# Softmax normalisation moved from the probabilities to a head pair's result, through DRAM; second query copies on GpSimd; squares of projections from SBUF

## The chip, the core and the metric

The kernel runs on one core of a Trainium2 chip. The metric is the device time of one execution in microseconds (us). A core has five engines with queues of their own that run in order: TensorE (PE in the profile, its weight loads PEld), VectorE (DVE), ScalarE (ACT), GpSimd (POOL) and SyncE (SP, which here only issues DMAs). They meet through semaphores. SBUF and PSUM are the on-chip memories; DRAM is reached by DMA alone.

## What is computed

Two layers of a streaming encoder over 512 tokens of width 1024. Each layer is a feed-forward block, a mixer and another feed-forward block. The mixer projects its input, runs two attention branches of 8 heads (A with a position bias, C with a forget bias) and a pooling branch, gates them and projects back. What matters here is one head of an attention branch:

```
logits = jnp.einsum('bqhd,bkhd->bhqk', qb, kf) + (cq[..., None] - cum_k[:, :, None, :])
logits = jnp.where(mask[None, None], logits, NEG_INF)
p = jax.nn.softmax(logits, axis=-1).astype(v.dtype)
return jnp.einsum('bhqk,bkhd->bqhd', p, v)
```

`qb` and `kf` are projections divided by their root mean square over the 64 elements of a head, so the squares of the projections are summed too.

## The kernel before, in words

All matrix products are made three times from values split into a high and a low part (`triple`, L117 to L122): a raw block comes in by DMA (`raw`), ACT writes the high part `whi` (L271), DVE the low part `wlo` (L273). Two raw buffers and three of `whi` and of `wlo` rotate. Tiles are taken from rings of a few buffers by tag: `t1` has 2, `t2` 3, `b` 17, PSUM has 4 banks named `mm` and 4 named `acc`. Whoever takes the next buffer of a ring waits until its last readers are done.

The program's order is made by a planner in the kernel: `later(delay, fn)` puts a task off until so many units of matmul work have been written out, and `poll` runs the tasks that are due. The order in which the instructions of each engine then stand is set when the program is built.

Attention (`attention`) goes over the heads h = 0..7, two heads to a pair p. For each head it writes four blocks of 128 queries, i = 0..3, and after each a piece of other work (`filler`): projections of branch C beside branch A, the gated merge of branch A beside branch C. One block is:

- `logits` (L945): two matmuls (L951, L952) into an `mm` bank; DVE adds bias or mask from the `strip` tile and finds the maximum (L955) into a `t1` tile; ACT takes the exponential into a `t2` tile `pr` with its row sum (L959); DVE inverts the sum (L961); `pr` is multiplied by it (L962), on POOL for i = 0..2 and on DVE for i = 3.
- `turn` (L965), 24 units later: PE transposes `pr` (L974) into an `mm` bank, ACT and DVE split it (L978, L979).
- `weigh` (L984), after each half of the queries, 14 units later: PE multiplies with the values (L996, L997); ACT copies the other half's rows into a `t1` tile (L1000), DVE adds (L1001), ACT and POOL split the sum into `y` (`split_to`, L378, L379), which a later merge multiplies.

The strips of the next head come by DMA and are finished on POOL: a memset in branch A (L926), an addition of the causal mask in branch C (L937).

Queries and keys come from `proj_qk`. As each of four PSUM banks `acc` is done, `evac` copies it (L826, ACT) and squares it (L828, ACT, from PSUM), and DVE sums the squares (L829). Later `turn` (L841) transposes one pair of heads into an `mm` bank; ACT writes the scaled rows (L853) and, for queries, writes them a second time to the other 64 partitions (L856); DVE makes the low part (L859); POOL fills the rest with zeros (L857).

Of the kernel before, what the change touches and what calls it, by code (L numbers as in the profile page):

```python
# [15 lines left out]
F32 = mybir.dt.float32  # L16
F32R = mybir.dt.float32r
I32 = mybir.dt.int32
AF = mybir.ActivationFunctionType
ALU = mybir.AluOpType  # L20
AX = mybir.AxisListType

P = 128
T = 512
# [6 lines left out]
HD = 64  # L31
NT = T // P
# [8 lines left out]
def encoder_kernel(tc, xT, c, w_ada, b_ada, gains, w_gate, w_up, w_down, w_qkv, w_f, w_ubg,  # L41
                   qk_gain, rel, fbias, w_pool, pool_scale, w_branch, w_out, inv_cnt, w_first, out):
    nc = tc.nc
# [10 lines left out]
    dr = open_pool(name="dr", bufs=1, space=bass.MemoryType.DRAM)  # L54
# [3 lines left out]
    NB, NRAW = 17, 2  # L58
# [5 lines left out]
    def st(shape, dt, tag, bufs):  # L64
        return sb.tile(shape, dt, tag=tag, bufs=bufs, name=nm(tag))
# [7 lines left out]
    def blk(tag, dt=F32R):  # L73
        bufs = {"xv": 4, "v2": 4, "b": NB}[tag]
        return st([P, 2, T], dt, tag, bufs)
# [22 lines left out]
    def later(delay, fn, group=None):  # L98
        t = Task(pe[0] + delay, fn, group)
        tasks.append(t)  # L100
        return t
# [33 lines left out]
    for b in range(4):  # L135
# [3 lines left out]
        sq = st([P, 2, T], F32, "wlo" if b else "whi", 3)  # L139
# [32 lines left out]

    x_dram = dr.tile([4, P, 2 * T], F32, name="x_dram")
    fv_dram = [dr.tile([H, FVLEN], F32, name=f"fv_dram{l}") for l in range(L)]

    last = {}

# [199 lines left out]
    def split_to(hi, lo, src, lo_eng=nc.vector):  # L377
        nc.scalar.copy(hi, src)  # L378
        lo_eng.tensor_tensor(lo, src, hi.bitcast(F32), op=ALU.subtract)  # L379
# [438 lines left out]
    def proj_qk(l, col, gcol, is_q, res, pre=None, norm=None):  # L818
        lows = []
        qs = []  # L820

        def evac(t, a):
            if t == 0:
                qs.extend((st([P, NT, T], F32, "ptb", 2), st([P, NT, H], F32, "qss", 1)))
            qn, ss = qs
            nc.scalar.copy(qn[:, t, :], a)  # L826
            sq = t2(T)
            nc.scalar.activation(sq, a, AF.Square)  # L828
            nc.vector.tensor_reduce(ss[:, t, :], sq.rearrange("p (h d) -> p h d", h=H), axis=AX.X, op=ALU.add)  # L829

        yield from proj(l, col, evac, pre, norm)
        qn, ss = qs
        v = st([P, NT * H], F32, "nt_v32", 2)
        nc.vector.tensor_scalar(v, ss.rearrange("p t h -> p (t h)"), 1.0 / HD, EPS, op0=ALU.mult, op1=ALU.add)
        r = rsqrt(v, NT * H)
        for t in range(NT):
            q3 = qn[:, t, :].rearrange("p (h d) -> p h d", h=H)
            eng = nc.vector if t % 2 else nc.gpsimd
            eng.tensor_tensor(q3, q3, r[:, t * H:(t + 1) * H].unsqueeze(2).to_broadcast([P, H, HD]), op=ALU.mult)

        def turn(p):  # L841
            pt = mmt()
            for t in range(NT):
                nc.tensor.transpose(pt[:, t * P:(t + 1) * P], qn[:, t, p * P:(p + 1) * P], ident)
            pe[0] += 2.2
            b = blk("b")
            if is_q:
                lows.append(blk("b"))
            first, second = slice(0, HD), slice(HD, P)
            for odd, (own, other) in enumerate(((first, second), (second, first))):  # L850
                dst = b[:, odd, :]
                gc = gcol[own, :]
                nc.scalar.activation(dst[own, :], pt[own, :], AF.Identity, scale=gc)  # L853
                low = dst[other, :]
                if is_q:
                    nc.scalar.activation(low, pt[own, :], AF.Identity, scale=gc)  # L856
                    nc.gpsimd.memset(lows[p][other, odd, :].bitcast(F32), 0.0)  # L857
                    low = lows[p][own, odd, :]
                nc.vector.scalar_tensor_tensor(low, pt[own, :], gc, dst[own, :].bitcast(F32),  # L859
                                               op0=ALU.mult, op1=ALU.subtract)  # L860
            res.append((b, lows[p]) if is_q else b)

        todo = [lambda p=p: turn(p) for p in range(4)]
        turns.append(todo)

        def ready(p):
            if len(todo) >= 4 - p:
                if heads[0] < (Q_GATE if is_q else K_GATE)[p]:
                    later(8, lambda: ready(p))
                else:  # L870
                    while len(todo) >= 4 - p:
                        todo.pop(0)()

        for p in range(4):
            later(TURN + 12 * p, lambda p=p: ready(p))
# [64 lines left out]
    def attention(qs, ks, vs, strip, ys, filler, budget, group):  # L940


        open_pt = {}

        def logits(h, i, strips):  # L945
            p, off = divmod(h, 2)
            (q, ql), k = qs[p], ks[p]
            odd = h % 2
            n = (i + 1) * P
            s = mmt()  # L950
            mm(s[:, :n], q[:, odd, i * P:(i + 1) * P], k[:, odd, :n], start=True, stop=False)  # L951
            mm(s[:, :n], ql[:, odd, i * P:(i + 1) * P], k[:, odd, :n], start=False, stop=True)  # L952
            lg = t1(T)[:, :n]
            mx = st([P, 1], F32, "mx", 4)
            nc.vector.tensor_tensor_reduce(out=lg, in0=s[:, :n], in1=strips[i], scale=-1.0, scalar=BIG,  # L955
                                           op0=ALU.add, op1=ALU.min, accum_out=mx)
            pr = t2(T)[:, :n]
            sm = st([P, 1], F32, "sm", 4)
            nc.scalar.activation(pr, lg, AF.Exp, bias=mx, scale=-1.0, accum_out=sm)  # L959
            rs = st([P, 1], F32, "rs", 4)  # L960
            nc.vector.reciprocal(rs, sm)  # L961
            (nc.vector if i == NT - 1 else nc.gpsimd).tensor_scalar(pr, pr, rs, None, op0=ALU.mult)  # L962
            pe[0] += 0.5 * (i + 1.5)
            later(LAG_T, lambda: turn(h, i, pr), group)

        def turn(h, i, pr):
            half, c = divmod(i, 2)
            nj = 2 * half + 2
            if c == 0:
                open_pt[h] = st([P, 2, nj, 256], F32R, "ptb" if half else "pta", 2 if half else 1)  # L970
            pt = open_pt[h]
            tp = mmt()
            for j in range(i + 1):
                nc.tensor.transpose(tp[:, j * P:(j + 1) * P], pr[:, j * P:(j + 1) * P], ident)  # L974
            tv = tp[:, :(i + 1) * P].rearrange("p (j q) -> p j q", q=P)
            dh = pt[:, 0, :i + 1, c * P:(c + 1) * P]
            dl = pt[:, 1, :i + 1, c * P:(c + 1) * P]
            nc.scalar.copy(dh, tv)  # L978
            nc.vector.tensor_tensor(dl, tv, dh.bitcast(F32), op=ALU.subtract)  # L979
            pe[0] += 0.55 * (i + 1)  # L980
            if c == 1:
                later(LAG_V, lambda: weigh(h, half, pt), group)

        def weigh(h, half, pt):  # L984
            p, off = divmod(h, 2)
            rows = slice(off * HD, off * HD + HD)
            other = slice(HD - off * HD, 2 * HD - off * HD)
            if off == 0 and half == 0:
                ys.append(blk("b"))
            y = ys[p]  # L990
            o = mmt((P, HALF))
            nj = 2 * half + 2
            for j in range(nj):
                q0 = P if j == nj - 1 else 0
                v2 = vs[j][:, h, :, :].rearrange("p a d -> p (a d)")
                mm(o[:, q0:], v2, pt[:, 0, j, q0:], start=(j == 0), stop=False)  # L996
                mm(o[:, q0:], v2, pt[:, 1, j, q0:], start=False, stop=(j == nj - 1))  # L997
            cols = slice(half * HALF, (half + 1) * HALF)
            yl = t1(T)[:, :HALF]
            nc.scalar.copy(yl[rows, :], o[other, :])  # L1000
            nc.vector.tensor_tensor(yl[rows, :], o[rows, :], yl[rows, :], op=ALU.add)  # L1001
            split_to(y[rows, 0, cols], y[rows, 1, cols], yl[rows, :], nc.gpsimd)
            pe[0] += 1.0 * nj

        for h in range(H):
            strips = strip(h)
            if group == "c":
                finish_turns(h // 2)
            for i in range(NT):
                logits(h, i, strips)  # L1010
                if i == NT - 1:
                    heads[0] = h + 1
                poll()
                goal = pe[0] + budget
                while filler is not None and pe[0] < goal:
                    if next(filler, "end") == "end":
                        filler = None
                poll()
        if filler is not None:
            for _ in filler:  # L1020
                pass

    LAG_T, LAG_V = 24, 14


    def pool_front(l, g):
# [244 lines left out]
```

## Time and profile before

| | us |
|---|---|
| median of 3 runs (lowest, highest) | 2454.31 (2453.69, 2454.6) |
| the profiled execution's own time | 2450.88 |
| its span, from the first to the last instruction | 2448.9 |
| attention of the first layer, stretch in the trace | 420 to 700 |
| attention of the second layer | 1620 to 1900 |

The profile's second part cuts the span into 40 equal slices of 61 us; a digit is the busy share of a slice in tenths.

```profile
PE   7999999999999999999999999999999999999999
DVE  8978766677643378787678656477765434765463
ACT  5333345677642353333453334366765333533341
POOL 3000002144532110000000000123354322000000
PEclk9999999999999999999999999999999999999999
```

The two stretches in which POOL is busy are the two mixers. An idle time in the profile is put down to the instruction that ended it, "engine tile line".

### The profile page before, as it was taken

What the parts mean: (1) busy time and instruction counts of PE and PEld (TensorE: products, weight loads), DVE (VectorE), ACT (ScalarE), POOL (GpSimd) and SP (SyncE); (2) the same over time, 40 slices, a digit from 0 to 9 for tenths busy, and PEclk for the clock granted to TensorE, in tenths of its full rate; (3) what the DMA queues carried; (4) which work ended last, traced back from release to release, by engine and by line L of the source; (5) the groups of instructions that cost most, each with busy time, mean ns of one, the idle gap of its engine ahead of it and who ended that gap; (6) DMA issues with size and microseconds to landing.
All of it is one profiled execution on the core that took longest, in us unless ns stands there. A gap on an engine that the chain in (4) does not pass through costs nothing. (4 is left out here: it accounts for less than half of the span.)

```text
span 2448.9 us, 34028 instructions
## 1 busy us (share of the span) xinstructions
PE 2396.8 (98%) x12966; PEld 2051.8 (84%) x12966; DVE 1600.5 (65%) x2859; ACT 1110.3 (45%) x1888; POOL 377.3 (15%) x439
## 2 busy tenths in 40 slices
PE   7999999999999999999999999999999999999999
PEld 5798888777888898988898888878777888988888
DVE  8978766677643378787678656477765434765463
ACT  5333345677642353333453334366765333533341
POOL 3000002144532110000000000123354322000000
PEclk9999999999999999999999999999999999999999
DMA  7756543222323426565327423223133234233232
GB/s 284 251 170 209 198 147 113 78 82 88 116 91 103 142 75 240 174 206 198 129 85 243 138 86 121 103 90 96 61 109 99 95 111 139 87 104 112 67 114 78
DMA packets 116279, 320.23 MB, mean 131 GB/s; under 512 B 11122, under 2 KB 13298, under 8 KB 116116
## 3 DMA queue, kind: packets, MB, share of 16 engines
q1 hardware_dynamic: 114962, 313.86, 38.3%
q0 software_dynamic: 1152, 4.19, 0.4%
q8 instruction: 102, 1.67, 0.3%
q14 instruction: 61, 0.50, 0.1%
q10 hardware_dynamic: 2, 0.00, 0.0%
HBM read 311.64 MB, written 6.38 MB: 130 GB/s over the span
## 5 line engine op out<-in xcount | busy, mean ns | idle before, releaser
L271 ACT CAST whi<-raw 128x1024 fp32r<-128x1024 f32 (+1 forms) x325 | 338.2, 1044 | 595.1 <-PE mm L120 289.2
L273 DVE TENSOR_TENSOR wlo<-raw,whi 128x1024 fp32r<-128x1024 f32 x317 | 392.2, 1240 | 197.4 <-ACT whi L271 194.2
L121 PE MATMUL mm<-hhi,wlo 128*128 128x512 f32 x744 | 289.8, 390 | 0.7 <-DVE wlo L273 0.4
L119 PE MATMUL mm<-hhi,whi 128*128 128x512 f32 x744 | 290.2, 390 | 0.0
L120 PE MATMUL mm<-hlo,whi 128*128 128x512 f32 x744 | 290.0, 390 | 0.0
L119 PE MATMUL acc<-b,whi 128*128 128x512 f32 (+1 forms) x704 | 264.1, 376 | 1.7 <-ACT b L378 1.7
L121 PE MATMUL acc<-b,wlo 128*128 128x512 f32 (+1 forms) x704 | 262.1, 374 | 3.5 <-DVE wlo L273 3.5
L120 PE MATMUL acc<-b,whi 128*128 128x512 f32 (+1 forms) x704 | 262.4, 373 | 0.0
L197 DVE CUSTOM_DVE_ANT_0 v<-v,b,badac 128x1024 f32<-128x1024 f32 x144 | 188.3, 1316 | 60.9 <-DMA v<-in_w_ada_dram 60.7
L119 PE MATMUL acc<-hhi,whi 128*128 128x512 f32 x480 | 190.7, 399 | 1.7 <-ACT hhi L738 1.7
L121 PE MATMUL acc<-hhi,wlo 128*128 128x512 f32 x480 | 188.9, 394 | 0.0
L120 PE MATMUL acc<-hlo,whi 128*128 128x512 f32 x480 | 188.5, 393 | 0.2 <-DVE hlo L741 0.2
L121 PEld LDWEIGHTS mm<-hhi,wlo 128*128 128x128 f32 x744 | 139.7, 188 | 30.9 <-DVE wlo L273 1.6
L119 PEld LDWEIGHTS mm<-hhi,whi 128*128 128x128 f32 x744 | 140.0, 188 | 27.9
L120 PEld LDWEIGHTS mm<-hlo,whi 128*128 128x128 f32 x744 | 139.7, 188 | 27.4
L121 PEld LDWEIGHTS acc<-b,wlo 128*128 128x128 f32 x704 | 133.8, 190 | 27.2 <-DVE wlo L273 4.6
L119 PEld LDWEIGHTS acc<-b,whi 128*128 128x128 f32 x704 | 133.3, 190 | 23.8 <-ACT b L378 2.6
L120 PEld LDWEIGHTS acc<-b,whi 128*128 128x128 f32 x704 | 133.3, 189 | 23.2 <-DVE b L379 0.9
L119 PE MATMUL acc<-whi,hhi 128*128 128x512 f32 x336 | 137.7, 411 | 4.4 <-ACT t L828 3.7
L120 PE MATMUL mm<-b,whi 128*128 128x512 f32 (+1 forms) x384 | 135.8, 354 | 0.0
L119 PE MATMUL mm<-b,whi 128*128 128x512 f32 (+1 forms) x384 | 135.8, 354 | 0.0
L121 PE MATMUL mm<-b,wlo 128*128 128x512 f32 (+1 forms) x384 | 135.6, 354 | 0.0
(300 smaller groups left out, 5598.3 us busy)
## 6 DMA issues: line engine op xcount, KB each, us to landing
v<-in_w_ada_dram SPq DMA_DIRECT2D x144, 512.0 KB, 4.4
raw<-in_w_down_dram SPq DMA_DIRECT2D x88, 512.0 KB, 3.5
raw<-in_w_up_dram SPq DMA_DIRECT2D x82, 512.0 KB, 3.4
b<-in_w_gate_dram SPq DMA_DIRECT2D x76, 512.0 KB, 5.3
raw<-in_w_ubg_dram SPq DMA_DIRECT2D x56, 512.0 KB, 3.3
raw<-in_w_qkv_dram SPq DMA_DIRECT2D x42, 512.0 KB, 3.7
raw<-in_w_branch_dram SPq DMA_DIRECT2D x24, 512.0 KB, 3.6
raw<-in_w_out_dram SPq DMA_DIRECT2D x16, 512.0 KB, 3.3
```

What stands on the lines that cost most here:

```text
L119: mm(o, lh, rh, start=start, stop=False, skip_group_check=onto)
L120: mm(o, lh, rl, start=False, stop=False, skip_group_check=onto)
L121: mm(o, ll, rh, start=False, stop=stop, skip_group_check=onto)
L197: dot = nc.vector.tensor_tensor_reduce(out=raw, in0=raw, in1=silc[0], scale=1.0, scalar=badac[:, l, j, d:d + 1], op0=ALU.mult, op1=ALU.add ...
L271: nc.scalar.copy(hi, raw)
L273: lo_eng.tensor_tensor(lo, raw, hi.bitcast(F32), op=ALU.subtract)
```

## The change

The probabilities are no longer divided by their sums. The four row sums of a head are kept in one tile, inverted together after the head's last block, and stored by a DMA from POOL into a DRAM row in the order of the queries (`inv_dram`, one row of 512 numbers for each head). A later task (`spread`, 50 units on) reads the row back by another DMA from POOL, repeated over the 64 partitions of that head, into the second half of a tile `rows_of` of the pair. `weigh` leaves its sum in the first half of that tile, unsplit. A last task for the pair (`norm_rows`, 36 units after the second head's `spread`) multiplies the two halves on DVE and splits the product on ACT and DVE.

Apart from that, the second copy of the queries is made by POOL from the first one in SBUF, and the squares are taken from the copy in SBUF.

```diff
+    inv_dram = {(g, p): dr.tile([2, T], F32, name=f"inv_dram_{g}{p}") for g in "ac" for p in range(4)}
...
             nc.scalar.copy(qn[:, t, :], a)
             sq = t2(T)
-            nc.scalar.activation(sq, a, AF.Square)
+            nc.scalar.activation(sq, qn[:, t, :], AF.Square)
...
                 if is_q:
-                    nc.scalar.activation(low, pt[own, :], AF.Identity, scale=gc)
+                    nc.gpsimd.tensor_copy(low, dst[own, :])
...
             pr = t2(T)[:, :n]
-            sm = st([P, 1], F32, "sm", 4)
-            nc.scalar.activation(pr, lg, AF.Exp, bias=mx, scale=-1.0, accum_out=sm)
-            rs = st([P, 1], F32, "rs", 4)
-            nc.vector.reciprocal(rs, sm)
-            (nc.vector if i == NT - 1 else nc.gpsimd).tensor_scalar(pr, pr, rs, None, op0=ALU.mult)
+            if i == 0:
+                sums[h] = st([P, NT], F32, "sm", 3)
+            nc.scalar.activation(pr, lg, AF.Exp, bias=mx, scale=-1.0, accum_out=sums[h][:, i:i + 1])
+            if i == NT - 1:
+                rs = st([P, NT], F32, "rs", 3)
+                nc.vector.reciprocal(rs, sums[h])
+                nc.gpsimd.dma_start(inv_dram[group, p][odd].rearrange("(i q) -> q i", q=P), rs)
+                later(LAG_R, lambda: spread(h), group)
...
             if off == 0 and half == 0:
-                ys.append(blk("b"))
-            y = ys[p]
+                rows_of[p] = st([P, 2, T], F32, "b", NB)
+            y = rows_of[p][:, 0, :]
...
             nc.scalar.copy(yl[rows, :], o[other, :])
-            nc.vector.tensor_tensor(yl[rows, :], o[rows, :], yl[rows, :], op=ALU.add)
-            split_to(y[rows, 0, cols], y[rows, 1, cols], yl[rows, :], nc.gpsimd)
+            nc.vector.tensor_tensor(y[rows, cols], o[rows, :], yl[rows, :], op=ALU.add)
             pe[0] += 1.0 * nj
+
+        def spread(h):
+            p, off = divmod(h, 2)
+            nc.gpsimd.dma_start(rows_of[p][off * HD:(off + 1) * HD, 1, :],
+                                inv_dram[group, p][off:off + 1, :].broadcast_to([HD, T]))
+            if off:
+                later(LAG_N, lambda: norm_rows(p), group)
+
+        def norm_rows(p):
+            y = blk("b")
+            ys.append(y)
+            full = rows_of[p][:, 0, :]
+            nc.vector.tensor_tensor(full, full, rows_of[p][:, 1, :], op=ALU.mult)
+            split_to(y[:, 0, :], y[:, 1, :], full)
...
-    LAG_T, LAG_V = 24, 14
+    LAG_T, LAG_V, LAG_R, LAG_N = 24, 14, 50, 36
```

How the instructions stand on the engines, at three places. Lines of the changed kernel are 1 higher than before up to the logits and 2 to 18 higher behind them. A name in brackets is what the instruction waits for (`DMASW` is a DMA issued by POOL, `DMAHW` one issued by SP).

First, POOL where branch A ends and branch C begins, in the first layer. Before, it scales the probabilities (`t`, L962) and splits results (`b`, L379) between the strips:

```order
L926 MEMSET strip_5329 64x64 [waits DMAHW7_49]
L962 TENSOR_SCALAR t_1019_5338<-t_1019_5338,rs_5341 128x128 [waits DVE_49,PE_49]
L962 TENSOR_SCALAR t_1025_5350<-t_1025_5350,rs_5353 128x256 [waits DVE_49,PE_49]
L937 TENSOR_TENSOR strip_5380<-strip_5380,cmask 128x128 [waits DMAHW2_49,DMAHW0_49]
L937 TENSOR_TENSOR strip_5380<-strip_5380,cmask 128x128 x2
L937 TENSOR_TENSOR ssum_5382<-ssum_5382,cmask 128x128 [waits DMAHW3_49,DMAHW1_49,PE_49]
L962 TENSOR_SCALAR t_1031_5362<-t_1031_5362,rs_5365 128x384 [waits DVE_49,Pool_49]
```

After the change, the store of head 6 (L966) stands ahead of the memset of head 7's strip (L927), and head 6's spread (L1011), which waits for that store, ahead of branch C's first strip (L938):

```order
L1011 DMA b_4893<-inv_dram_a_125 64x512 [waits DMASW6_49]
L966 DMA inv_dram_a_126<-rs_5222 128x4x1 [waits DVE_49]
L927 MEMSET strip_5241 64x64 [waits DMAHW7_49,Pool_49]
L1011 DMA b_5225<-inv_dram_a_126 64x512 [waits DMASW1_49,DMASW3_49,DMASW0_49,Activation_49]
L938 TENSOR_TENSOR strip_5280<-strip_5280,cmask 128x128 [waits DMAHW2_49,DMAHW0_49]
L938 TENSOR_TENSOR strip_5280<-strip_5280,cmask 128x128 x2
L938 TENSOR_TENSOR ssum_5282<-ssum_5282,cmask 128x128 [waits DMAHW3_49,DMAHW1_49,PE_49]
```

What moved: nothing of POOL's stands between PE's logits and PE's transposes any more, but the strips now stand behind DMAs.

Second, DVE in branch C of the first layer, around the last block of a head. Before, the inverse (L961) and the scaling (L962) of every block stand between the logits of the next ones:

```order
L1001 TENSOR_TENSOR t_1218_6007<-mm_5998,t_1218_6007 64x256 [waits DVE_49,Activation_49]
L955 ISA t_1221_6023,mx_6024<-mm_6020,ssum_5900 128x512 [waits DMAHW5_49,DVE_49,PE_49]
L955 ISA mx_6024 128x1
L979 TENSOR_TENSOR pta_5987<-mm_6015,pta_5987 128x2x128 [waits Activation_49]
L273 TENSOR_TENSOR wlo_6097<-raw_6094,whi_6096 128x1024 [waits DMAHW3_49,PE_49,Activation_49]
L961 RECIPROCAL rs_6029<-sm_6027 128x1 [waits Activation_49]
L962 TENSOR_SCALAR t_1223_6026<-t_1223_6026,rs_6029 128x512 [waits DVE_49]
```

After, a pair's multiplication (L1020) stands one head behind the inverse of the pair's second head, ahead of a split of transposed probabilities (L984) and of the next head's last logits (L957):

```order
L1006 TENSOR_TENSOR b_5780<-mm_5993,t_1191_6002 64x256 [waits Activation_49]
L1020 TENSOR_TENSOR b_5780<-b_5780 128x512 [waits DMASW3_49,DMASW1_49,DVE_49]
L984 TENSOR_TENSOR pta_5982<-mm_6008,pta_5982 128x2x128 [waits Activation_49]
L957 ISA t_1194_6017,mx_6018<-mm_6014,ssum_5904 128x512 [waits DMAHW0_49,PE_49,Pool_49]
L957 ISA mx_6018 128x1
L274 TENSOR_TENSOR wlo_6221<-raw_6218,whi_6220 128x1024 [waits DMAHW1_49,PE_49,Activation_49]
L965 RECIPROCAL rs_6022<-sm_5917 128x4 [waits DMASW6_49,Activation_49]
```

What moved: DVE loses three small instructions and one scaling for each head, and gains, for each pair, one instruction that waits for two DMAs.

Third, ACT where the first queries are turned while the keys' banks come off PE, first layer. Before:

```order
L853 ACTIVATE b_3726<-mm_3721,qg_117 64x512 [waits PE_49]
L856 ACTIVATE b_3726<-mm_3721,qg_117 64x512
L826 COPY ptb_3742<-acc_3639 128x512 [waits PE_49]
L828 ACTIVATE t_607_3745<-acc_3639 128x512 [waits DVE_49]
L853 ACTIVATE b_3726<-mm_3721,qg_117 64x512 [waits DVE_49]
L856 ACTIVATE b_3726<-mm_3721,qg_117 64x512
L853 ACTIVATE b_3756<-mm_3751,qg_117 64x512 [waits PE_49]
```

After:

```order
L854 ACTIVATE b_3734<-mm_3729,qg_117 64x512 [waits PE_49]
L827 COPY ptb_3750<-acc_3647 128x512 [waits PE_49]
L854 ACTIVATE b_3734<-mm_3729,qg_117 64x512 [waits DVE_49]
L829 ACTIVATE t_607_3753<-ptb_3750 128x512 [waits Activation_49]
L854 ACTIVATE b_3764<-mm_3759,qg_117 64x512 [waits PE_49]
L827 COPY ptb_3750<-acc_3648 128x512 [waits PE_49]
```

What moved: the two second copies are gone from ACT, and the bank `acc` has its last reader in the COPY, one instruction earlier; the square may stand behind the next turn.

More of the change, by code (lines that the diff above doesn't have):

```diff
@@ L943, in attention @@
         open_pt = {}
+        sums, rows_of = {}, {}
         def logits(h, i, strips):
```

## The prediction, made before the changed kernel had run

> **What bounds the kernel now.** I read the page's totals first, then the stretches of the two attention phases, then what PE waited for.
>
> ```profile
> span 2448.9 us, 34028 instructions
> PE 2396.8 (98%) x12966; PEld 2051.8 (84%) x12966; DVE 1600.5 (65%) x2859; ACT 1110.3 (45%) x1888; POOL 377.3 (15%) x439
> ```
>
> PE is busy for all but 2448.9 - 2396.8 = 52.1 us. The change neither adds nor removes a matmul or a transpose, so it can only win from those 52.1 us, and the question is where they lie. The table of stretches gives the length, then the busy time of PE, PEld, DVE, ACT and POOL, the granted clock and DMA:
>
> ```profile
> 420.00:700.00 280.00, 266.70 (x1371) 215.57 (x1370) 190.85 (x463) 186.28 (x398) 113.12 (x152) 0.99 0.30 92
> 1620.00:1900.00 280.00, 265.05 (x1364) 212.92 (x1363) 193.38 (x472) 183.90 (x394) 113.25 (x148) 1.00 0.30 90
> ```
>
> PE idles 13.3 us in the first layer's attention and 15.0 us in the second's, 28.3 us together. The rest lies mostly at the program's start (the first slice of the page's row for PE is at 7 tenths), which the change leaves alone. No other engine is full there: DVE is busy 68% and ACT 67% of the time. So the idle time is a matter of single late links, and the list of PE's waits (total, times, longest) names them:
>
> ```profile
> PE mm L974 <- POOL t L962: 6.8, 15, 0.7
> PE mm L951 <- DVE t L1001: 4.6, 6, 1.1
> ...
> PE acc L119 <- ACT t L828: 3.7, 6, 1.3
> ...
> PE mm L951 <- DVE ptb L979: 3.0, 2, 1.5
> PE mm L951 <- DVE b L859: 1.8, 2, 0.9
> PE mm L951 <- DVE mx L955: 1.8, 4, 0.7
> ...
> PE mm L974 <- DVE ptb L979: 1.7, 4, 0.5
> ...
> PE mm L997 <- DVE ptb L979: 1.2, 4, 0.3
> PE mm L974 <- DVE rs L961: 1.0, 2, 0.5
> ...
> PE mm L974 <- DVE b L859: 0.5, 2, 0.3
> ```
>
> These ten rows sum to 26.1 us, which is about the ceiling of any gain: 1.1% of the run.
>
> **The change part by part.** Groups of instructions by line, with busy time and mean duration in ns, price what goes and comes (POOL, then ACT, then DVE):
>
> ```profile
> L962 POOL TENSOR_SCALAR t<-t,rs 128x128 f32<-128x128 f32 (+2 forms) x96 | 88.7, 927 | 138.2 <-DVE rs L961 117.7 <-PE acc L121 5.7 <-PE mm L974 5.7
> L379 POOL TENSOR_TENSOR b<-t,b 64x256 fp32r<-64x256 f32 x64 | 56.4, 882 | 94.5 <-ACT b L378 93.4
> ...
> L857 POOL MEMSET b<- 64x512 f32 x32 | 17.2, 537 | 1.4
> ...
> L1119 POOL DMA_DIRECT2D x_dram<-xv x8 | 4.8, 603 | 647.7 <-DVE xv L430 647.3
> ...
> L378 ACT CAST b<-t 64x256 fp32r<-64x256 f32 x64 | 25.9, 404 | 26.7 <-DVE t L1001 26.3
> ...
> L856 ACT ACTIVATE b<-mm,qg 64x512 fp32r<-64x512 f32 x32 | 21.9, 684 | 0.4
> ...
> L378 ACT CAST strip<-ssum 128x512 fp32r<-128x512 f32 x35 | 21.7, 620 | 36.4 <-DVE ssum L541 36.4
> ...
> L828 ACT ACTIVATE t<-acc 128x512 f32<-128x512 f32 x32 | 19.1, 598 | 0.0
> ...
> L541 DVE TENSOR_TENSOR ssum<-b,b 128x512 f32<-128x512 f32 x35 | 23.9, 683 | 0.1
> ...
> L961 DVE RECIPROCAL rs<-sm 128x1 f32<-128x1 f32 x128 | 20.2, 159 | 37.7 <-ACT t L959 37.6
> ...
> L962 DVE TENSOR_SCALAR t<-t,rs 128x512 f32<-128x512 f32 x32 | 16.6, 520 | 1.2
> ```
>
> Over both layers DVE loses the 32 scalings (16.6 us) and 96 of 128 inverses (15.1) and gains for 16 pairs a multiplication and a low part, both of the form of L541 (16 x 2 x 0.683 = 21.9): 9.8 us less. ACT loses 64 casts (25.9) and 32 second copies (21.9) and gains 16 casts of 128x512 (16 x 0.620 = 9.9): 37.9 us less. Reading the squares from SBUF is not in the trace for this line; ACT's 0.620 for 128x512 from SBUF against 0.598 from PSUM bounds it at plus 0.7 us over 32, and I take that. POOL loses 145.1 us and gains 32 copies of 64x512, which the trace does not show: a memset of that shape takes 0.537, its additions on 64x256 0.882, so 0.54 to 1.76; I take 0.7, nearer to the memset since one operand is read, 22 us in all. It gains 64 DMA issues too, 0.60 each by the row of L1119, which sends 128 long rows. The store sends 512 single numbers; scaled with their count it would be 2.4 us. Between 0.6 and 2.4 I take 1. None of this busy time is on PE's path by itself. What counts is which wait of the list goes:
>
> (a) Transposes behind the scaling, 6.8 + 1.0 us. The transposes will wait for ACT's exponential, ready an inverse (0.159) and a scaling (0.520 on DVE, 0.927 on POOL) earlier: 0.7 to 1.1 us. The longest wait was 0.7, so all 7.8 us go. What would be late next is the exponential itself.
>
> (b) Projections behind the square, 3.7 us. The bank comes free with the COPY, one instruction of 0.598 earlier, and in branch A's query turn, where the longest wait of 1.3 lies, the square was held behind two copies and a wait on DVE; I take 3.0.
>
> (c) Low parts of queries, 1.8 + 0.5 us. DVE waited for the second copy L856 (0.684 each), which leaves ACT: 2.0 of 2.3. Logits of branch A's first head need POOL's copies now, but many values are projected between them and the logits, so this costs nothing; without that cover a copy and its memset would cost 1.2 us, once per layer.
>
> (d) Logits behind L1001 and behind the maximum, 4.6 + 1.8 us. The timeline (start, duration, idle time before) shows one such wait:
>
> ```profile
> 593.24 0.72 POOL L379 TENSOR_TENSOR b<-t,b 64x256 fp32r<-64x256 f32 x1
> ...
> 594.00 0.36 ACT L1000 COPY t<-mm 64x256 f32<-64x256 f32 x1 [0.98 <-POOL b L379]
> ...
> 594.39 0.43 DVE L1001 TENSOR_TENSOR t<-mm,t 64x256 f32<-64x256 f32 x1 [1.58 <-ACT t L1000]
> ...
> 594.88 0.33 PE L951 MATMUL mm<-b,b 128*128 128x128 f32 x1 [0.64 <-DVE t L1001]
> ```
>
> POOL's split held a `t1` buffer, ACT's copy had to wait for it, DVE for ACT, and PE for DVE. That split is gone. The other half of (d), above all the longest, 1.1, has other causes (DVE sits in the forget gate's work); I take 3.5 of 6.4.
>
> (e) Splits of transposed probabilities, 3.0 + 1.7 + 1.2 us. Their causes stay; DVE comes to them a scaling of 0.52 earlier at the two longest: 1.0 of 5.9.
>
> Together 17.3 us. Two things go the other way. At the end of branch A the store of head 6 stands ahead of the memset of head 7's strip, for which DVE already waited:
>
> ```profile
> 577.12 0.14 POOL L926 MEMSET strip<- 64x64 f32 x1
> ...
> 577.29 0.29 DVE L955 CUSTOM_DVE_ANT_0 t<-mm,strip 128x128 f32<-128x128 f32 x1 [0.99 <-POOL strip L926]
> ```
>
> I add 0.7 us a layer (0 to 2.4, the issue's range), 1.4 in all. And when a link comes earlier, PE reaches the next late one earlier: I give back a quarter of 17.3, about 4. (A choice: the list leaves 26.1 - 17.3 = 8.8 us of waits standing that can grow.) Net: 17.3 - 1.4 - 4 = 12 us.
>
> **The new wait.** DVE's multiplication waits for store and spread. In branch C it stands one head behind the inverse; the trace has an inverse of the last block and the next head's last L1001 at
>
> ```profile
> 666.99 0.16 DVE L961 RECIPROCAL rs<-sm 128x1 f32<-128x1 f32 x1
> ...
> 675.38 0.42 DVE L1001 TENSOR_TENSOR t<-mm,t 64x256 f32<-64x256 f32 x1 [1.21 <-ACT t L1000]
> ...
> 679.04 0.15 DVE L961 RECIPROCAL rs<-sm 128x1 f32<-128x1 f32 x1
> ...
> 685.15 0.43 DVE L1001 TENSOR_TENSOR t<-mm,t 64x256 f32<-64x256 f32 x1 [1.86 <-ACT t L1000]
> ```
>
> so the cover is 675.8 - 667.0 = 8.8 us, and 6.5 us for the last pair. Landing times from issue (KB, us):
>
> ```profile
> x_dram<-xv POOLq DMA_DIRECT2D x8, 512.0 KB, 3.2
> ...
> ssum<-fv_dram SPq DMA_DIRECT2D x16, 256.0 KB, 3.1
> ...
> out_dram<-xv SPq DMA_DIRECT2D x8, 128.0 KB, 1.7
> ...
> qkgc<-in_qk_gain_dram SPq DMA_DIRECT2D x1, 4.0 KB, 4.3
> ```
>
> The store is small and scattered, like the last row: 1.7 to 4.3, I take 4.3. The spread is a repeated row of 128 KB: 1.7 to 3.1, I take 3.1. Together 7.4 us, at most 2.4 + 4.3 + 0.6 + 3.1 = 10.4. At 7.4 only the last pair is late, by 0.9 us; on PE 60 projections follow whose weights are split already, and behind branch C the stretches show PE full:
>
> ```profile
> 690.00:720.00 30.00, 30.00 (x134) 24.75 (x132) 14.09 (x25) 10.99 (x16) 14.52 (x20) 1.00 0.27 88
> ```
>
> 134 matmuls in 30 us are 0.224 each, so 60 cover 13.4 us, and the late pair costs nothing. Behind the waiting DVE stand the next split L979, the logits L955 and `wlo`, and PE behind them.
>
> The Trainium skill's page "DMA: Bandwidth & Descriptors" speaks against the store (Rules for kernel authors: a strided last dim lowers to one descriptor per element, so rearrange it; Bandwidth, Measured: about 10.5 ns per packet). With its fixed 2.0 us per DMA (Anatomy of one DMA), an estimate by that page is 2.0 + 512 x 0.0105 = 7.4 us for the store and 2.3 for the spread, 9.7 us; by it two pairs of branch C in each layer would be 0.9 us late and the forecast 2 to 4 us higher. No row here shows such a store.
>
> **The rivals.** *Given back*: PE's waits only change their releaser; the transposes wait for the exponential, which itself waits for DVE. For it: 8.8 us of waits stay, and DVE's load falls by only 9.8 us. Against it: the shorter links of (a) exceed every wait they replace. Then a quarter of 17.3 remains, minus 1.4: 3 us faster. *All goes*: DVE and ACT, with 48 us less to do, are early everywhere; 22 of 26.1 us go. *Late round trip*, the slower one: store and spread take 18 us instead of 7.4. The multiplication then holds DVE in branch C for 18 - 8.8 = 9.2 us at the first three pairs of each layer, 55 us in all (the last pair has PE's 13.4 us of cover, branch A's heads are longer and are left out). DVE is two thirds busy, and I let half reach PE: 28 us lost against 12 won, 16 us slower. It decides where half the hold reaches 12 us: 4 us at each of six pairs, so from a round trip of 12.8 us on. For it: no store of 512 single numbers is in this trace. Against it: the bound of 10.4.
>
> **How the numbers follow.** The profiled execution took 2450.88 us, its span plus 2.0; the median of the runs is 2454.31, 3.4 higher. Net 12 gives 2438.9 for a profiled execution and 2442.3 against the median, which is what I forecast. Chances: forecast (5 to 17 us faster, 2437 to 2449) 0.55; all goes (2430 to 2437) 0.13; given back (2449 to 2459, about 2451) 0.19; late round trip (above 2459, about 2470) 0.13. A measurement of this kernel can tell about 0.2% from no change, 4.9 us: faster 0.68, same 0.19, slower 0.13. The range 2433 to 2459 leaves out half of "all goes" and the loss.
>
> **What would show it.** PE's waits on POOL at the transposes gone and PE's idle time in the two attention stretches 10 to 20 us in all instead of 28.3; waits on L829 near zero; no idle time of DVE ended by a DMA ahead of L1020 except before the last pair; stores landing within 4.3 us. It is wrong if DVE idles ahead of L1020 for several us at each pair, if the store's issue on POOL takes more than 2.4 us, or if the transposes wait for L960 as long as they did for L962.

## The result and the profile after

| | us, median (lowest to highest) |
|---|---|
| before, measured beside it, 4 runs | 2454.0 (2451.65 to 2454.6) |
| after, 4 runs | 2563.49 (2563.04 to 2567.3) |
| ratio, with its 95% interval | 1.0451 (1.0433 to 1.047) |

The change makes the kernel 4.5% slower. The forecast was 12 us faster, and the time lies 104 us above its range. Up to the logits the changed kernel's line numbers are one to two higher than before. The page's totals and row for the granted clock, after:

```profile
span 2561.3 us, 33707 instructions
PE 2422.0 (95%) x12966; PEld 2077.9 (81%) x12966; DVE 1590.8 (62%) x2763; ACT 1072.0 (42%) x1808; POOL 289.1 (11%) x375
PEclk9999999998889999999999999999978999999999
```

DVE, ACT and POOL have less to do, as intended. PE does the same 12966 instructions, but idles 2561.3 - 2422.0 = 139.3 us in place of 52.1, and is busy 25.2 us longer. Most of both belongs to the two attentions. The table of stretches (length; busy PE, PEld, DVE, ACT, POOL; granted clock; DMA) has, first for the windows of before and then for windows that last until the slower attentions end:

```profile
420.00:700.00 280.00, 236.18 (x1170) 194.16 (x1169) 162.75 (x370) 148.18 (x320) 59.14 (x100) 0.91 0.39 85
1620.00:1900.00 280.00, 252.77 (x1305) 210.20 (x1304) 178.88 (x402) 155.33 (x315) 62.35 (x96) 0.96 0.41 91
...
420.00:760.00 340.00, 285.77 (x1383) 233.65 (x1381) 184.93 (x415) 167.37 (x359) 67.70 (x117) 0.90 0.37 82
1665.00:2015.00 350.00, 295.69 (x1457) 242.68 (x1456) 196.52 (x435) 173.83 (x367) 69.62 (x116) 0.92 0.42 82
```

In the windows of before PE idles 43.8 and 27.2 us, where it was 13.3 and 15.0; but they miss much of the second attention, which now begins and ends later. In the wider ones it idles 54.2 and 54.3 us, together 108.5 of the 139.3. The clock granted to PE is 0.90 and 0.92 there, where it was 0.99 and 1.00, and a matmul is busy for 0.205 us on average in place of 0.194; elsewhere it is 0.182 in both kernels. DVE's row for the new multiplication (busy, mean ns | idle before it) says what it waits for:

```profile
L1020 DVE TENSOR_TENSOR b<-b 128x512 f32<-128x512 f32 x16 | 11.1, 692 | 133.7 <-DMA b<-inv_dram_c 83.8 <-DMA b<-inv_dram_a 49.9
```

All 16 multiplications wait for the spread, 8.4 us each on average. DMA issues after (KB, median us from issue to landing), and then the row of before for the strips of branch C:

```profile
strip<-fv_dram SPq DMA_DIRECT2D x16, 384.0 KB, 11.0
...
ssum<-fv_dram SPq DMA_DIRECT2D x16, 256.0 KB, 5.6
...
b<-inv_dram_a POOLq DMA_DIRECT2D x16, 128.0 KB, 5.8
b<-inv_dram_c POOLq DMA_DIRECT2D x16, 128.0 KB, 4.8
...
inv_dram_a<-rs POOLq DMA_DIRECT2D x16, 2.0 KB, 10.2
inv_dram_c<-rs POOLq DMA_DIRECT2D x16, 2.0 KB, 10.1
```

```profile
strip<-fv_dram SPq DMA_DIRECT2D x16, 384.0 KB, 3.6
```

The store of 2 KB takes 10 us, and strips on SP's queue, which the change does not touch, take 11.0 in place of 3.6. One pair of branch C in the timeline of after (start, duration, idle before it) shows how it adds up:

```profile
692.88 0.17 DVE L965 RECIPROCAL rs<-sm 128x4 f32<-128x4 f32 x1
...
695.25 2.28 POOL L938 TENSOR_TENSOR strip<-strip,cmask 128x128 f32<-128x128 f32 x3 [3.66 <-DMA strip<-fv_dram]
697.48 0.79 POOL L966 DMA_DIRECT2D inv_dram_c<-rs  x1
...
701.26 0.43 DVE L1006 TENSOR_TENSOR b<-mm,t 64x256 f32<-64x256 f32 x1 [2.05 <-ACT t L1005]
706.96 0.53 POOL L1011 DMA_DIRECT2D b<-inv_dram_c  x1 [8.20 <-DMA inv_dram_c<-rs]
...
710.39 0.69 DVE L1020 TENSOR_TENSOR b<-b 128x512 f32<-128x512 f32 x1 [8.70 <-DMA b<-inv_dram_c]
```

The inverse is there at 692.9. POOL, in order, still waits for a late strip, adds the mask to it (2.3 us) and issues the store 4.6 us after the inverse. The spread can be issued 9.5 us after that, and the multiplication starts 3.4 us after the spread: 17.5 us in all. DVE was there at 701.7, 8.8 us after the inverse, which is the cover that the prediction had read. The rest, 8.7 us, DVE stands still. Over all 16 pairs the way from the inverse to the multiplication takes 15.3 to 22.7 us, of which DVE's own work covers 5.9 to 12.1. With DVE the splits and maxima stand still that PE needs, and the exponentials behind the maxima; these four rows of PE's waits (total, times, longest) make 92.6 of its 139.3 us:

```profile
PE mm L979 <- DVE mx L957: 32.8, 4, 13.9
PE mm L1001 <- DVE pta L984: 25.3, 4, 6.8
PE mm L979 <- ACT t L962: 17.9, 2, 9.1
PE mm L1002 <- DVE pta L984: 16.6, 6, 4.0
```

### The profile page after: what moved, and what is told of

Its sections match the earlier page's. It is cut to its first block, busy times and chain, and to the rows that moved or that the text cites. A ratio compares the mean times of both kernels' runs of the same rounds, so it can differ in the third digit from the quotient of the medians.

```text
span 2561.3 us, 33707 instructions
## 1 busy us (share of the span) xinstructions
PE 2422.0 (95%) x12966; PEld 2077.9 (81%) x12966; DVE 1590.8 (62%) x2763; ACT 1072.0 (42%) x1808; POOL 289.1 (11%) x375
## 5 line engine op out<-in xcount | busy, mean ns | idle before, releaser
L119 PE MATMUL acc<-hhi,whi 128*128 128x512 f32 x480 | 195.9, 409 | 8.7 <-ACT whi L272 7.0
L962 ACT ACTIVATE t<-t,mx 128x128 f32<-128x128 f32 (+3 forms) x128 | 71.9, 562 | 156.0 <-DVE mx L957 133.3
```

The lines of the kernel that those rows point to most:

```text
L119: mm(o, lh, rh, start=start, stop=False, skip_group_check=onto)
```

## The experiments

Differences in us are against the kernel before as measured in the same job, by medians (2449.9, 2451.7 and 2449.4 in the three jobs, 2454.0 beside the changed kernel). The changed kernel stands at +109.5.

| kernel | median us | against before | ratio (95%) |
|---|---|---|---|
| e1: query copies and squares alone | 2441.1 | -8.8 | 0.9962 (0.9947 to 0.9976) |
| e2: no trip, not normalised | 2417.5 | -32.4 | 0.9866 (0.9852 to 0.9881) |
| e3: store in 128 pieces | 2423.8 | -26.1 | 0.9892 (0.9878 to 0.9907) |
| e4: LAG_N 80 | 2557.0 | +107.1 | 1.0432 (1.0415 to 1.045) |
| e6: store, but no spread, not normalised | 2462.1 | +10.4 | 1.0048 (1.0033 to 1.0063) |
| e7: multiplication tied later | 2497.8 | +46.1 | 1.0191 (1.0176 to 1.0206) |
| e8: store issued by ACT | 2535.5 | +83.8 | 1.0342 (1.0325 to 1.0359) |
| e9: 128 pieces, tied later | 2415.6 | -36.1 | 0.9856 (0.9842 to 0.9871) |
| e10: no trip, scaling kept | 2425.8 | -23.7 | 0.99 (0.9884 to 0.9917) |
| e11: store in 256 pieces | 2442.4 | -7.0 | 0.9972 (0.9959 to 0.9986) |

**Parts without the trip (e1, e2, e10).** e1 makes two edits in the kernel before:

```
-            nc.scalar.activation(sq, a, AF.Square)
+            nc.scalar.activation(sq, qn[:, t, :], AF.Square)
...
-                    nc.scalar.activation(low, pt[own, :], AF.Identity, scale=gc)
+                    nc.gpsimd.tensor_copy(low, dst[own, :])
```

> The kernel before with two parts of the change alone: Square of projections from SBUF and the second query copies on GpSimd; softmax scaling as before, no round trip through DRAM. Theory 'trip' (the loss is all in the round trip of the inverse sums): terms (b) and (c) of the prediction appear, PE's waits on the squares and on the low parts of the queries go, 3 to 6 us faster than before, 2448 to 2452. Rival 'parts' (the copies on GpSimd, now in the way of strips and of scaling, cost): 2460 or more, with PE waiting for POOL more than the 6.8 us of before.

e2 takes the store and the spread out of the changed kernel:

```
-                nc.gpsimd.dma_start(inv_dram[group, p][odd].rearrange("(i q) -> q i", q=P), rs)
...
-            nc.gpsimd.dma_start(rows_of[p][off * HD:(off + 1) * HD, 1, :],
-                                inv_dram[group, p][off:off + 1, :].broadcast_to([HD, T]))
...
-            nc.vector.tensor_tensor(full, full, rows_of[p][:, 1, :], op=ALU.mult)
+            nc.vector.tensor_tensor(full, full, ones[:, 0:1].to_broadcast([P, T]), op=ALU.mult)
```

> The changed kernel without the store and without the spread: nothing goes through DRAM, and the multiplication at its place takes ones in place of the inverse row sums, so the output is not normalised. All instructions of PE, ACT and DVE stay. Theory 'trip': the loss is gone and the on-record gain appears, 2437 to 2444. Rival 'place' (the one more b buffer held per pair, or the multiplication and split that now stand in one piece on DVE and ACT, cost): 2460 or more, with PE's waits on DVE mx and pta still tens of us.

e10 takes out the same and the multiplication, and has the scaling of before again:

```
+            (nc.vector if i == NT - 1 else nc.gpsimd).tensor_scalar(pr, pr, rs, None, op0=ALU.mult)
```

> No trip, and the scaling of the probabilities by their inverse sums kept as in the kernel before (GpSimd for three blocks of four, DVE for the fourth); the rest as in the changed kernel: query copies, squares, and a pair's result added unsplit and split later in one piece by ACT and DVE. Its output is normalised. It lies between the two-parts kernel (2441.1), which it exceeds by terms (d) and (e) of the prediction, 4.5 us, and the kernel without trip or scaling (2417.5), which has term (a), 7.8 us, besides. By the prediction's terms: 2436 to 2438, that is (a) is worth less than twice the others. If the scaling on GpSimd alone is what made the 24 us between the two: 2436 to 2442. If the split of y on GpSimd was: 2418 to 2428.

e1 gained 8.8 us, more than the 3 to 6 expected; e2 32.4, more than any case of the prediction and below the band of its own expectation; both say that the loss is in the trip and nowhere else. e10 lies nearer to e2 than to e1, outside both of the expectations that went by (a) and inside the third, which put the gain down to the split of `y` on POOL: taking the scaling off the probabilities, with the new multiplication counted in, is worth 32.4 - 23.7 = 8.7 us, the later and unsplit sum of a pair 23.7 - 8.8 = 14.9. Totals of e2:

```profile
span 2415.4 us, 33569 instructions
PE 2383.0 (99%) x12966; PEld 2051.0 (85%) x12966; DVE 1594.8 (66%) x2763; ACT 1071.9 (44%) x1808; POOL 248.5 (10%) x311
```

PE's idle time fell from 52.1 to 32.4 us, which is 19.7 of the 33.5 by which the span fell. The other 13.8 us came out of its busy time, with the same 12966 instructions.

**Pieces of the store (e3, e11, e8).** e3 stores a head's 512 numbers in the order in which they lie in SBUF, four to a partition, and lets the multiplication read them with a stride:

```
-                nc.gpsimd.dma_start(inv_dram[group, p][odd].rearrange("(i q) -> q i", q=P), rs)
+                nc.gpsimd.dma_start(inv_dram[group, p][odd].rearrange("(q i) -> q i", i=NT), rs)
...
+            inv = rows_of[p][:, 1, :].rearrange("p (q i) -> p i q", i=NT)
```

> The changed kernel, with each head's row of inverse sums stored in the order (query, block): 128 pieces of 16 bytes in place of 512 single numbers; the multiplication reads the spread row with a stride of four numbers, same result. Theory 'scatter' (the 10.1 us of the store are the 512 single numbers): the store lands in 2 to 4.3 us, the spread in 3 to 4, the waits of DVE ahead of the multiplication fall from 133.7 to below 40 us, 2440 to 2470. Rival 'fixed' (a store and a load of DRAM one behind the other take that long whatever their pieces): the store still lands in 8 us or more and the time stays above 2530. Rival 'strided' (the strided reading slows the multiplication): its 692 ns become over 1000.

e11 does the same with two numbers to a piece, in the order "(j q i) -> q j i" with i of 2.

> The store in 256 pieces of 8 bytes (two blocks' numbers side by side), between the 512 pieces of 4 bytes of the changed kernel (lands in 10.1 us, 2563.5) and 128 of 16 bytes (1.8 in branch A and 3.2 in branch C, 2423.8). If each piece costs its own time: lands in about 5 us (2.5 + 128 x 0.02), the strips from fv_dram in 4 to 7, and the time lies well below the middle, 2430 to 2470, because most of the chain is then covered. Rival: what is slow is a piece below some size and not their number, and 8 bytes are below it as well: lands in 8 us or more and strips stay near 10, 2500 or more.

e8 leaves the 512 pieces and changes the queue:

```
-                nc.gpsimd.dma_start(inv_dram[group, p][odd].rearrange("(i q) -> q i", q=P), rs)
+                nc.scalar.dma_start(inv_dram[group, p][odd].rearrange("(i q) -> q i", q=P), rs)
```

> The changed kernel with the same store of 512 single numbers issued by ACT in place of GpSimd. Theory 'transfer' (the 10.1 us are the 512 pieces on the DMA engines): it lands in 8 to 12 us from ACT's queue too, and the time stays above 2530. Rival 'queue' (they are GpSimd's way of issuing, which makes the pieces in software): it lands in 2 to 5 us, and the time falls to 2425 to 2460.

DMA issues of e3, then e11, then e8, where the last row is the count of packets in ACT's queue (packets, MB, share):

```profile
strip<-fv_dram SPq DMA_DIRECT2D x16, 384.0 KB, 3.7
...
inv_dram_a<-rs POOLq DMA_DIRECT2D x16, 2.0 KB, 1.8
inv_dram_c<-rs POOLq DMA_DIRECT2D x16, 2.0 KB, 3.2
```

```profile
strip<-fv_dram SPq DMA_DIRECT2D x16, 384.0 KB, 5.0
...
inv_dram_a<-rs POOLq DMA_DIRECT2D x16, 2.0 KB, 4.1
inv_dram_c<-rs POOLq DMA_DIRECT2D x16, 2.0 KB, 4.9
```

```profile
strip<-fv_dram SPq DMA_DIRECT2D x16, 384.0 KB, 8.7
...
inv_dram_a<-rs ACTq DMA_DIRECT2D x16, 2.0 KB, 9.3
inv_dram_c<-rs ACTq DMA_DIRECT2D x16, 2.0 KB, 10.4
...
q10 hardware_dynamic: 16898, 0.07, 0.4%
```

The same 2 KB take 1.8 and 3.2 us in 128 pieces, 4.1 and 4.9 in 256, 10.2 and 10.1 in 512, and nearly as long in 512 pieces from ACT's queue. The first theory of each of the three runs holds in its landing times: it is the pieces. If each has its own time, that is (4.9 - 3.2) / 128 = 13 ns to (10.2 - 4.1) / 256 = 24 ns, an estimate from these rows. Since the store keeps its 2 KB, the pieces get smaller as they get more; the runs do not tell the number of pieces from their size. In ACT's queue, which held 2 packets before, they can be counted: 16896 for 32 stores, 528 each. GpSimd's way of issuing is not the cause. e8 is 25.7 us below the changed kernel all the same; DVE's waits at the multiplication are 24.6 us shorter there (109.1 in place of 133.7). That fits a store which no longer queues behind POOL's strips, but was not tested apart. In e3 the waits at the multiplication fell from 133.7 to 13.2 us; its time lies below the band, which counted on the prediction's gain and not on e2's:

```profile
DVE b L1021 <- DMA b<-inv_dram_c: 12.4, 6, 4.8
...
DVE b L1021 <- DMA b<-inv_dram_a: 0.8, 1, 0.8
```

The strided multiplication has its price, as its rival said, but a small one: 1100 ns with a stride of four numbers in e3, 710 with two in e11, against 692, on 16 of them.

**What the store does to others (e6).** The store stays, nobody reads it; the spread is taken out and the multiplication takes ones as in e2.

> The changed kernel with the store of 512 single numbers as it is, but without the spread: nobody reads the stored row, the multiplication takes ones, so the output is not normalised. Theory 'chain' (the loss is the wait for store and spread): with nobody waiting, the store may land as late as it likes; about the 2417.5 of the kernel without the trip, 2417 to 2430. Rival 'neighbour' (the store's 512 pieces keep the strips' loads off the DMA engines, and late strips hold the logits by themselves): the strips still land in 9 to 11 us instead of 3.6, DVE waits for strips, 2450 or more.

It came out at 2462.1, inside what "neighbour" said and far outside "chain". The DMA issues of e6, and then the row of SP's queue (packets, MB, share of 16 engines' span), first of before and then of e6:

```profile
strip<-fv_dram SPq DMA_DIRECT2D x16, 384.0 KB, 10.4
...
ssum<-fv_dram SPq DMA_DIRECT2D x16, 256.0 KB, 8.8
```

```profile
q1 hardware_dynamic: 114962, 313.86, 38.3%
```

```profile
q1 hardware_dynamic: 114962, 313.86, 41.5%
```

SP moves the same bytes in the same packets, but they occupy the engines for 41.5% of 2459.4 us in place of 38.3% of 2448.9: 1020.7 against 937.9, 83 us more of all sixteen. With nothing waiting for the store, 32 of them still cost 10.4 + 32.4 = 42.8 us against e2. It is not that POOL has to issue them: e3 issues as many, and its strips land in 3.7 us. DVE waits 22.2 us for strips that POOL finishes late, where it waited 2.1 in e2:

```profile
DVE t L957 <- POOL ssum L938: 11.5, 7, 5.0
DVE t L957 <- POOL strip L938: 10.7, 2, 7.8
```

How much of the 42.8 us these waits make is not shown. SP's loads of raw weights are late too: they land at 15.2 us at the longest in e6 and 7.4 before. The totals of e6 say where PE loses the time:

```profile
span 2459.4 us, 33640 instructions
PE 2399.5 (98%) x12966; PEld 2061.7 (84%) x12966; DVE 1593.1 (65%) x2763; ACT 1072.1 (44%) x1808; POOL 272.0 (11%) x343
```

It idles 59.9 us in place of 32.4 in e2, and is busy 16.5 us longer; the clock granted to it in the attention stretches is 0.96 and 0.99, in e2 1.00 in both.

**Who is held (e4, e7, e9).** e4 sets LAG_N to 80 in the changed kernel, nothing else.

> The changed kernel with LAG_N 80 in place of 36: store and spread where they are, the multiplication 44 units (some 10 us) later in the program. Theory 'DVE held' (DVE, waiting in order at the multiplication, keeps logits and splits from PE): DVE's waits there fall from 133.7 to below 30 us and the time to 2450 to 2480. Rival 'POOL held' (POOL, waiting at the spread for the store, keeps the strips from the logits): the waits at the multiplication fall as well, but POOL's 149 us at the spread stay, DVE waits for strips instead, and the time stays above 2520.

Neither theory got its test: the time and the waits (129.6 us at the multiplication) stay as they were, because the edit moved almost nothing. In the trace the multiplication keeps its row among DVE's 2763 instructions at 14 of 16 places, and at the first pair of branch C in each layer it stands three rows earlier; a delay of the planner sets when an instruction is written out, not where it ends up on its engine. e7 ties it down, behind the logits' instruction that was written last when the program comes to it:

```
+            seen[0] = nc.vector.tensor_tensor_reduce(out=lg, in0=s[:, :n], in1=strips[i], scale=-1.0, scalar=BIG,
...
-            nc.vector.tensor_tensor(full, full, rows_of[p][:, 1, :], op=ALU.mult)
+            with tc.issue_after(seen[0].ins):
+                nc.vector.tensor_tensor(full, full, rows_of[p][:, 1, :], op=ALU.mult)
...
-    LAG_T, LAG_V, LAG_R, LAG_N = 24, 14, 50, 36
+    LAG_T, LAG_V, LAG_R, LAG_N = 24, 14, 50, 60
```

> The changed kernel, slow store and all, with the multiplication now really later on DVE: it is tied behind the logits' instruction that DVE has at hand when the program reaches it, and LAG_N is 60; at three pairs of each branch it stands about 17 to 24 DVE instructions (some half a pair, 11 us) later than in the changed kernel, the last pair of each branch stays. Theory 'DVE held': DVE's waits at the multiplication fall from 133.7 to below 40 us, and the time to 2435 to 2475. Rival 'POOL held' (POOL, waiting for the store at the spread, delays strips and the next store whatever DVE does): POOL's 149 us at the spread stay, DVE waits for strips instead, above 2520.

The waits of DVE, and then of POOL, in e7:

```profile
DVE b L1022 <- DMA b<-inv_dram_c: 39.9, 6, 12.1
...
DVE b L1022 <- DMA b<-inv_dram_a: 19.6, 3, 10.1
```

```profile
POOL b L1012 <- DMA inv_dram_a<-rs: 95.2, 14, 9.5
POOL b L1012 <- DMA inv_dram_c<-rs: 57.2, 6, 10.3
```

DVE's fell by 133.7 - 59.5 = 74.2 us, and the time by 109.5 - 46.1 = 63.4, while POOL's waits at the spread for the store did not fall (149.1 us in the changed kernel, 95.2 + 57.2 = 152.4 in e7). So "DVE held" is the larger part of what reading the row back costs; "POOL held" is not, except as a link that makes the store late. Both bands were missed: e7 still pays the 42.8 us that e6 shows, and 59.5 us of waits remain, 41.4 of them at the last pair of each branch, which the tie does not move.

e9 is e3 with the tie and LAG_N 60 of e7.

> The store in 128 pieces of 16 bytes as in the contiguous version (2423.8), with the multiplication tied later as in the pinned one, LAG_N 60. If DVE's 13.2 us of waits at the multiplication are what still lies between the contiguous version and the one without a trip (2417.5), they go and the time is 2417 to 2422. Rival: the difference is the store's and spread's issue on POOL and their traffic, or the later multiplication makes the merge or a buffer late: 2423 or more.

```profile
span 2415.9 us, 33709 instructions
PE 2384.1 (99%) x12966; PEld 2053.1 (85%) x12966; DVE 1598.9 (66%) x2763; ACT 1073.1 (44%) x1808; POOL 287.3 (12%) x375
```

Waits at the multiplication are down from 13.2 to 8.0 us, and the time by 10 us against its own before (-36.1 and -26.1), more than these waits; it lies below both of its expectations, and what else it gained is open. e9 is the fastest kernel with a normalised output: 1.4% faster than before, at the level of e2, which has no trip at all. So no cost of the trip can be seen once its store has few pieces and its reader stands late enough; a kernel without the trip and with the later multiplication, the stricter comparison, was not run.

## Why the prediction was wrong

The 109.5 us are a gain of 32.4 (e2), a loss of 42.8 by the store's pieces in other loads (e6 against e2), and a loss of 109.5 - 10.4 = 99.1 by reading the row back (changed kernel against e6). Of the last, e7 got back 63.4 by moving the multiplication alone. The rest stands beside the 59.5 us of DVE's waits that e7 has left, and was not taken apart; e3 and e9 have the same spreads, and no such loss.

- **The step that failed** is the price of the store: "small and scattered, like the last row: 1.7 to 4.3, I take 4.3". It landed in 10.1. The row beside it, 4 KB in 4.3 us, said nothing of 512 pieces, and the nearest row was taken for an upper end. With the spread at 4.8 to 5.8 in place of 3.1, the trip of 7.4 us, "at most 10.4", was 17.5 in the pair shown and never below 15.3.
- **The Trainium skill**, "DMA: Bandwidth & Descriptors" (Rules for kernel authors), was right in kind: a strided last dim is one descriptor per element, and e3, which rearranges it as the Trainium skill says, shows 1.8 to 3.2 us in place of 10.1. Its 10.5 ns per packet (Bandwidth, Measured), by which the prediction had 7.4 us as an estimate, was measured on loads into SBUF; for this store it is short, since the runs show 13 to 24 ns. With the prediction's own covers, its estimate of 9.7 us makes three pairs of branch C in each layer 0.9 us late, and not two.
- **POOL's queue** had no term. The prediction priced the store's issue (1 us taken, 0.79 measured), but not that the store stands behind a strip for which POOL waits: 4.6 us in the pair shown, and 1.2 to 7.9 at eight of the 16 pairs. At the others the store is issued within 0.7 us, and the way still takes 15.3 us or more, so this term comes second to the store's landing.
- **The neighbours** had no term either. The prediction asked what waits for the store, not what shares the DMA engines with it: 42.8 us.
- **The cover** was read rightly: in the changed kernel DVE reaches the multiplication 8.8 to 8.9 us after the inverse at the second and third pair of branch C (8.8 read) and 6.2 at the last (6.5 read).
- **"I let half reach PE"** was wrong. In e7, 74.2 us less of waiting on DVE were 63.4 us less of time. And branch A, left out because its heads are longer, has 49.9 of the 133.7 us: DVE's work covers 10.6 to 12.1 us there, and the way takes 15.3 to 20.9. The rival *late round trip* named the mechanism, its place and nearly its size, 18 us and a hold of 9.2, but counted 6 holds of 16 at half and came to 2470, 93 us too low. Its 18 us came from no row, so that they fit is luck.
- **The gain** was sized too small: 17.3 us, less 5.4. Scaling (a): 7.8 expected, 8.7 measured. Squares and low parts (b, c): 5.0 and 8.8. Sums and splits (d, e): 4.5 and 14.9, the largest miss. In PE's idle time alone the three are 4.8 (e10 to e2), 5.4 (before to e1) and 9.5 (e1 to e10), together 19.7: the waits as a whole were sized well, (a) too large and (d, e) too small. The ceiling of 26.1 us from PE's list of waits was none, since 13.8 us also came out of busy time, which the prediction put at nothing; why, the runs do not show. Nothing of the quarter given back can be seen in e2.
- **The small prices** held: a query copy on POOL 0.61 us (0.7 taken), a square from SBUF 0.627 against 0.598 (0.620 taken):

```profile
L829 ACT ACTIVATE t<-ptb 128x512 f32<-128x512 f32 x32 | 20.1, 627 | 0.4
L857 POOL CAST b<-b 64x512 fp32r<-64x512 f32 x32 | 19.4, 608 | 15.5 <-ACT b L854 14.5
```

- **What would show it** was named rightly: DVE idles ahead of L1020 at each pair, and the stores do not land within 4.3 us. The transposes wait for the exponential too (L962 after, which the prediction calls L960), 17.9 us in two waits; in e2 that row is gone, so it is the hold on DVE again and not the missing scaling.

## What to carry to other kernels

Before a small result goes through DRAM, count the pieces of the transfer, not its bytes, and ask which loads share the engines with them; an order in which the numbers already lie in SBUF, undone by a strided read later, took the store from 10.1 us to 3.2 and the kernel from 4.5% slower to 1.1% faster. A consumer of such a trip belongs as far behind it as the whole chain takes, with the wait in front of the issuing queue counted in, and where it stands is to be read from the built order and not from a delay in the program. A load of 62% did not give DVE slack for an in-order wait, because the next matmuls hang on what stands behind it.

## What the runs showed of the hardware that was not expected

- A store of 2 KB in 512 pieces of 4 bytes took 10.1 us, in 256 pieces 4.1 to 4.9, in 128 pieces 1.8 to 3.2; in 512 pieces from ACT's queue it took 9.3 to 10.4, so the queue mattered little.
- Such a store slows the loads of another queue: strips of 384 KB landed in 10.4 us in place of 3.6 (e6).
- A multiplication of 128x512 on DVE whose second operand is read with a stride of four numbers took 1100 ns, with a stride of two 710, without 692.
